# Strassen for the right half of two row blocks, streamed with B, and the loads and norms moved to make room

One Trainium2 chip, one core. The metric is the device time of one execution in microseconds (us), medians over runs. Engines go by the names that the profile gives them: PE does matrix products (TensorE), DVE and ACT work on vectors (VectorE and ScalarE), POOL and SP here mostly issue DMA transfers, that is loads and stores (GpSimd and SyncE). SBUF is the on-chip memory, PSUM the banks into which PE writes its products; copying a bank out to SBUF is called eviction. A norm is the work on a row block of A from its squares to its scale factor. Each normalized block is cast to fp16, then transposed. L and a number is a line of the kernel.

## The reference

```python
m, k, n = 2048, 2048, 2048          # a, b: float32 normal; gamma: float32; eps = 1e-5
x = np.matmul(a, b)
rms = np.sqrt(np.mean(x ** 2, axis=-1, keepdims=True) + eps)
return (gamma * x / rms).astype(np.float32)
```

## The kernel before

Rows are worked in 16 blocks of 128, columns in 4 chunks of 512. A matmul here is always one 128x128 stationary block against 512 columns, so a plain chunk of a row block costs 16 of them (the depth of 2048 in steps of 128).

- *Left half* (to about 39.8 us): row blocks 0 to 3 times the left 1024 columns, plainly, while A and the left half of B arrive in eight pieces. A PE transpose turns each piece of A.
- *Right half* (to about 69 us): the same four row blocks times the right 1024 columns, while the right half of B arrives. 4 rows x 2 chunks x 16 = 128 matmuls.
- *Groups*: the other 12 row blocks in pairs. A pair and two column chunks make a 2x2 problem with all of B in place, so one level of Strassen's scheme (7 products of half-size blocks in place of 8, at the price of extra sums) serves: 7 products of 8 matmuls, 56, in place of 64 plain ones. DVE makes the sums of A, of B and of the products; ACT evicts, squares, and normalizes the next blocks of A to fp16; DMA transposes those.

The stream of the right half and the list of loads of the kernel before:

```python
later = ([("b", kp) for kp in range(5)]                 # pieces of the right half of B
         + [("a", HB), ("b", 5), ("b", 6), ("a", HB + 1), ("b", 7)])   # and blocks 4, 5 of A
# ...
groups2 = [(r, c) for r in range(HB) for c in (2, 3)][:-1]   # 7 chunks stream, the 8th follows
for kp in range(KP):
    load_later(1)
    # ... transposes of block 4 in steps 6 and 7
    stream(groups2, kp, before)                 # 14 plain matmuls per piece of B
    square(squares[kp][0], x_chunk(*squares[kp]))
    # ... norm and fp16 of blocks 4, 5 after steps 4 and 6; sums of B for the groups
```

One product of a group, and the buffers: PSUM has 7 banks for these; a row's output lives in one of 8 SBUF buffers, reused group after group.

```python
p2, p5 = new_bank(), new_bank()
product(g, j, 2, p2)
nc.scalar.copy(out=c, in_=p2)          # c is in the output buffer: waits for its last store
product(g, j, 5, p5)
nc.vector.tensor_tensor(out=t, in0=p5, in1=c, op=ALU.add)
# ... product 1
product(g, j, 4, p2, start=False)      # goes on top of p2: waits for the copy
product(g, j, 3, p5, start=False)      # goes on top of p5: waits for the sum t
```

Of the kernel before, what the change touches and what calls it, by code (L numbers as in the profile page):

```python
# [17 lines left out]
def kernel(  # L18
# [13 lines left out]
    nc = tc.nc  # L32
# [18 lines left out]
    stat_pool = ctx.enter_context(tc.tile_pool(name="stat_pool", bufs=8))  # L51
# [25 lines left out]
    spare = head_at.rearrange("p t r m -> p (t r m)")[:, K:2 * K].bitcast(FP32)[:, 0:CH]  # L77

    def a16_slot(mb):

        if mb < HB + 2:
            return x_slot[HB + 1 + 2 * (mb % 2)].bitcast(FP16)
        flat = head_at.rearrange("p t r m -> p (t r m)").bitcast(FP16)
        return flat[:, (2 + mb % 2) * K:(3 + mb % 2) * K]
# [27 lines left out]

    def load_block(mb):
        a32[mb] = a_pool.tile([P, K], FP32, name="a32")
        nc.gpsimd.dma_start(out=a32[mb], in_=a[mb * P:(mb + 1) * P, :])
# [8 lines left out]
    identity_f = consts.tile([P, P], FP32, name="identity_f")  # L124
# [4 lines left out]
    nc.vector.memset(warm, 0.0)  # L129
    identity = consts.tile([P, P], BF16, name="identity")  # L130
# [43 lines left out]
    def transpose_half(mb, g):  # L174
        bank = ps_t.tile([P, CH], FP32, name="tbank")
# [7 lines left out]
        nc.vector.tensor_copy(out=at(mb)[:, g * 8:(g + 1) * 8, :], in_=view)  # L183
# [8 lines left out]
    def new_msq(mb):  # L192
        msq[mb] = stat_pool.tile([P, NCH + 1], FP32, name="msq")
        n_sq[mb] = 0

    for mb in range(HB):
        new_msq(mb)
        nc.gpsimd.memset(msq[mb][:, NCH:], float(eps))
# [27 lines left out]
    def row_apply(mb):  # L226
        a16[mb] = a16_slot(mb)
        if mb < HB + 2:
            nc.vector.tensor_scalar_mul(out=a16[mb], in0=a32.pop(mb), scalar1=factor.pop(mb))
# [5 lines left out]
    def quarter(g, r, c):  # L235
        return at(2 * g + r)[:, c::2, :]

    def a_sums(g, which):
# [3 lines left out]
        for s in which:  # L242
            x, y, op = terms[s]
            nc.vector.tensor_tensor(out=s_sum[s], in0=x, in1=y, op=op)  # L244
# [11 lines left out]
    def b_sum_7(j, kp):  # L256

        b21, b22 = (b_quarter(j, kp, 1, c) for c in range(2))
        nc.vector.tensor_tensor(out=b21, in0=b21, in1=b22, op=ALU.add)

    def b_sum_6(j, kp):

        b11, b12 = (b_quarter(j, kp, 0, c) for c in range(2))
        nc.vector.tensor_tensor(out=b12, in0=b12, in1=b11, op=ALU.add)

# [6 lines left out]
    def product(g, j, m, bank, start=True):  # L272
        for kp in range(KP):
            lhsT = {3: quarter(g, 0, 0), 4: quarter(g, 1, 1)}[m] if m in (3, 4) else s_sum[m]
            rhs = {1: lambda: sums[j][:, 0, kp, :], 2: lambda: b_quarter(j, kp, 0, 0),
                   3: lambda: sums[j][:, 1, kp, :], 4: lambda: sums[j][:, 2, kp, :],
                   5: lambda: b_quarter(j, kp, 1, 1), 6: lambda: b_quarter(j, kp, 0, 1),
                   7: lambda: b_quarter(j, kp, 1, 0)}[m]()
            nc.tensor.matmul(bank, lhsT[:, kp, :], rhs,  # L279
                             start=(start and kp == 0), stop=(kp == KP - 1),  # L280
                             skip_group_check=not start)
# [5 lines left out]
    def square(mb, src):  # L287
# [3 lines left out]
        nc.scalar.activation(out=sq[:, 0:CH], in_=src, func=ACTF.Square,  # L291
                             scale=inv_sqrt_n, accum_out=msq[mb][:, c:c + 1])
# [40 lines left out]

    def finish(mb, order=(0, 1)):
        if mb not in rms_of:
            take_rms(mb)
        r = inverse(rms_of.pop(mb))
        for h in order:
            x = x_half.pop((mb, h))
            nc.vector.scalar_tensor_tensor(  # L340
                out=x, in0=x, scalar=r, in1=gamma_sb[:, h * HALF:(h + 1) * HALF],
                op0=ALU.mult, op1=ALU.mult)
# [394 lines left out]
```

## Time and profile before

| | before |
|---|---|
| time, median (range) | 224.41 us (224.26 to 225.11) |
| span of the profiled run | 222.6 us |
| left half, right half, groups, tail (us, read from PE's timeline) | 7.7 to 39.84, to 69.25, to 214.7, to 222.6 |

The page of the kernel before: busy time of an engine, tenths of busy time in 40 slices of 5.6 us, and the chain that ended last.

```profile
...
PE 211.1 (95%) x1043; PEld 98.6 (44%) x1043; DVE 161.8 (73%) x324; ACT 129.1 (58%) x272; POOL 24.5 (11%) x49
...
PE   7899999999999999999999999999999999999950
...
DVE  2427557983999989978949298837994589587692
...
PE 83%; DMA 8%; DVE 2%; POOL 2%; issue 1%; ACT 1%; DVEq 0%; ACTq 0%; POOLq 0%
...
```

PE is full in nearly every slice and makes up 83% of the chain. But its busy share alone proves little: the mean matmul is shown as 379 ns long, though they start 216 ns apart. How long PE really idles is seen in the stretches and the timeline. The view by stretches (start:end, then busy us of PE, its weight load, DVE, ACT, POOL, and granted clock, DMA share, GB/s):

```profile
...
core 0: us, PE busy (x) PEld busy (x) DVE busy (x) ACT busy (x) POOL busy (x), PEclk, DMA share, GB/s
7.00:39.80 32.80, 31.84 (x190) 16.04 (x189) 18.37 (x39) 3.16 (x6) 11.33 (x17) 1.00 1.21 208
39.80:69.20 29.40, 29.40 (x161) 14.30 (x160) 24.18 (x59) 19.38 (x43) 2.34 (x4) 1.00 1.00 284
69.20:93.50 24.30, 24.30 (x113) 10.95 (x112) 22.90 (x49) 19.01 (x42) 1.24 (x3) 1.00 0.70 226
93.50:214.70 121.20, 121.18 (x570) 55.50 (x568) 91.52 (x169) 83.64 (x174) 3.71 (x9) 1.00 0.62 193
214.70:222.60 7.90, 0.00 (x0) 0.00 (x0) 3.26 (x7) 2.04 (x7) 0.00 (x0) 0.79 0.60 209
...
```

From 39.8 to 214.7 us the view shows no idle time on PE; in the last stretch (the tail) it has nothing left to do. The waits of PE inside the stream (for whom, total us, times, longest):

```profile
...
PE acc L350 <- DMA b<-in_b_dram: 0.4, 1, 0.4
PE tbank L382 <- DVE head_at L170: 0.4, 1, 0.4
```

0.8 us in all. PE's timeline (start, duration, line and operation, count):

```profile
...
39.84 19.80 PE L350 MATMUL acc<-b,head_at 128*128 128x512 bf16 x91
59.48 0.61 PE L179 MATMUL tbank<-identity_h,x 128*128 128x128 f16 x8
...
67.09 2.32 PE L350 MATMUL acc<-b,head_at 128*128 128x512 bf16 x10
69.25 3.62 PE L279 MATMUL acc<-b,s 128*128 128x512 bf16 x16
72.70 1.89 PE L279 MATMUL acc<-t_left,s 128*128 128x512 bf16 x8
...
212.77 1.91 PE L677 MATMUL acc<-b,s 128*128 128x256 bf16 x16
```

The 91 matmuls from 39.84 us end, start to start, at 59.48: 19.64/91 = 0.2158 us each. The last line is the last product. The Trainium skill's page "TensorE: Matmul & The Clock Gate", section "Back-to-back issue gap", gives about 216 ns for the isolated gap at 512 columns and about 131 ns as a sustained figure; this trace shows 216 in a stream without gaps, and 131 nowhere.

### The profile page before, as it was taken

How to read it: one execution, taken by the hardware profiler on the slowest of the kernel's cores; microseconds unless marked ns; L12 is line 12 of the kernel's file. 1: busy time of each engine (PE TensorE's matmuls, PEld its weight loads, DVE VectorE, ACT ScalarE, POOL GpSimd, SP SyncE). 2: the span in 40 equal slices, each digit the busy share in tenths (PEclk: the TensorE clock that was granted, in tenths of full speed). 3: DMA queues.
4: the chain of work that ended last, by engine and by line, in shares of the span. 5: the costliest groups of instructions: out<-in, count | busy, mean ns of one | idle time of the engine just before them, and what ended most of it. 6: DMA issues, size and time to landing. Idle time of an engine off the chain costs nothing.

```text
span 222.6 us, 3026 instructions
## 1 busy us (share of the span) xinstructions
PE 211.1 (95%) x1043; PEld 98.6 (44%) x1043; DVE 161.8 (73%) x324; ACT 129.1 (58%) x272; POOL 24.5 (11%) x49
## 2 busy tenths in 40 slices
PE   7899999999999999999999999999999999999950
PEld 2445444444454444444444444444444444444430
DVE  2427557983999989978949298837994589587692
ACT  3110002807698895799646985699478954334570
POOL 7534232300000001000100002000200000000000
PEclk9999999999999999999999999999999999999997
DMA  6999999999973499818889259945994794044045
GB/s 184 223 202 209 203 208 211 212 303 259 327 280 159 188 272 292 310 72 226 276 228 400 58 174 222 366 151 143 246 368 168 97 282 189 0 188 193 0 190 188
DMA packets 36176, 47.13 MB, mean 212 GB/s; under 512 B 21952, under 2 KB 26048, under 8 KB 34496
## 3 DMA queue, kind: packets, MB, share of 16 engines
q0 software_dynamic: 9648, 23.33, 41.6%
q1 hardware_dynamic: 26080, 22.29, 33.0%
q10 hardware_dynamic: 432, 1.31, 2.0%
q8 instruction: 8, 0.13, 0.2%
q14 instruction: 8, 0.07, 0.1%
HBM read 34.60 MB, written 16.78 MB: 231 GB/s over the span
## 4 chain that ended last, share of the span: by engine, by line
PE 83%; DMA 8%; DVE 2%; POOL 2%; issue 1%; ACT 1%; DVEq 0%; ACTq 0%; POOLq 0%
PE acc L279 63%; PE acc L350 18%; DMA b<-in_b_dram 8%; POOL early L106 1%; DVE x L617 1%; POOL b L100 1%; DVE x L620 1%; PE tbank L179 1%; PE tbank L382 1%; PE tbank L165 1%; ACT sq L291 0%; DVEq L732 0%; ACT sq L682 0%; DVE x L690 0%; DVE r L322 0%
## 5 line engine op out<-in xcount | busy, mean ns | idle before, releaser
L279 PE MATMUL acc<-b,s 128*128 128x512 bf16 x376 | 83.3, 379 | 0.0
L279 PEld LDWEIGHTS <-s 128*128 128x128 f16 x472 | 46.2, 98 | 55.7 <-DVE s L244 0.2
L350 PE MATMUL acc<-b,head_at 128*128 128x512 bf16 x240 | 55.1, 379 | 0.6 <-DMA b<-in_b_dram 0.4
L291 ACT ACTIVATE sq<-x 128x512 bf16<-128x512 f32 x62 | 39.1, 631 | 10.9 <-DVE x L520 5.1
L340 DVE SCALAR_TENSOR_TENSOR x<-x,r,gamma_sb 128x1024 f32<-128x1024 f32 x28 | 34.7, 1282 | 0.8
L209 ACT ACTIVATE sq<-a 128x1024 bf16<-128x1024 f32 x24 | 25.4, 1057 | 16.8 <-DMA a<-in_a_dram 16.4
L350 PEld LDWEIGHTS <-head_at 128*128 128x128 bf16 x240 | 22.9, 98 | 26.7 <-issue 1.1
L393 ACT COPY x<-acc 128x512 f32<-128x512 f32 x11 | 5.9, 591 | 25.1 <-PE acc L350 25.1
L231 ACT ACTIVATE head_at<-a,s 128x2048 f16<-128x2048 f32 x10 | 19.9, 1990 | 0.0
L279 PEld LDWEIGHTS <-at_even 128*128 128x128 f16 x96 | 9.4, 98 | 11.5 <-issue 0.4
L279 PEld LDWEIGHTS <-head_at 128*128 128x128 f16 x96 | 9.4, 98 | 11.3
L100 POOL DMA_DIRECT2D b<-in_b_dram x15 | 10.6, 708 | 16.0 <-DMA b<-in_b_dram 13.2
L217 DVE TENSOR_SCALAR s<-norm 128x1 f32<-128x1 f32 x12 | 1.8, 150 | 14.3 <-ACT norm L212 14.2
L244 DVE TENSOR_TENSOR s<-at_even 128x1024 f16<-128x1024 f16 x15 | 9.7, 684 | 2.8 <-DMA at_even<-head_at 2.8
L291 ACT ACTIVATION_READ_ACCUMULATOR sq<-x 128x1 f32 x62 | 11.7, 188 | 0.0
L279 PE MATMUL acc<-t_left,s 128*128 128x512 bf16 x48 | 11.3, 379 | 0.0
L279 PE MATMUL acc<-early,s 128*128 128x512 bf16 x48 | 11.3, 379 | 0.0
L279 PE MATMUL acc<-early,at_even 128*128 128x512 bf16 x48 | 11.0, 379 | 0.0
L279 PE MATMUL acc<-t_left,at_even 128*128 128x512 bf16 x48 | 10.9, 379 | 0.0
L509 ACT COPY x<-acc 128x512 f32<-128x512 f32 x10 | 5.7, 575 | 8.9 <-PE acc L279 8.9
L279 PE MATMUL acc<-t_left,head_at 128*128 128x512 bf16 x48 | 10.8, 379 | 0.0
L279 PE MATMUL acc<-early,head_at 128*128 128x512 bf16 x48 | 10.8, 379 | 0.0
(86 smaller groups left out, 205.8 us busy)
## 6 DMA issues: line engine op xcount, KB each, us to landing
out_dram<-x SPq DMA_DIRECT2D x30, 512.0 KB, 3.1
a<-in_a_dram POOLq DMA_DIRECT2D x12, 1024.0 KB, 8.5
b<-in_b_dram POOLq DMA_DIRECT2D x15, 512.0 KB, 17.1
early<-in_a_dram POOLq DMA_DIRECT2D x7, 256.0 KB, 14.8
early<-in_b_dram ACTq DMA_DIRECT2D x2, 512.0 KB, 5.9
gamma_sb<-in_gamma_dram POOLq DMA_DIRECT2D x1, 1024.0 KB, 19.9
out_dram<-x SPq DMA_DIRECT2D x3, 256.0 KB, 3.5
early<-in_a_dram SPq DMA_DIRECT2D x1, 512.0 KB, 5.7
```

Of the source, the lines that this page charges most:

```text
L100: nc.gpsimd.dma_start(out=raw[j][kp], in_=b[kp * W2:(kp + 1) * W2, j * HALF:(j + 1) * HALF].rearrange("(t p) n -> p t n", p=P))
L106: nc.gpsimd.dma_start(out=ah(kp), in_=a[0:HB * P, kp * W2:(kp + 1) * W2].rearrange("(r p) k -> p r k", p=P))
L165: nc.tensor.matmul(view[:, t, r, :], ah(kp)[:, r, t * P:(t + 1) * P], identity, is_transpose=True, start=(t == 0 and r == 0), stop=(t == 1 ...
L209: nc.scalar.activation(out=junk, in_=a32[mb][:, h * HALF:(h + 1) * HALF], func=ACTF.Square, scale=2.0 ** -8, accum_out=n2[:, h:h + 1])
L231: nc.scalar.activation(out=a16[mb], in_=a32.pop(mb), func=ACTF.Copy, scale=factor.pop(mb))
L244: nc.vector.tensor_tensor(out=s_sum[s], in0=x, in1=y, op=op)
L279: nc.tensor.matmul(bank, lhsT[:, kp, :], rhs, start=(start and kp == 0), stop=(kp == KP - 1), skip_group_check=not start)
L291: nc.scalar.activation(out=sq[:, 0:CH], in_=src, func=ACTF.Square, scale=inv_sqrt_n, accum_out=msq[mb][:, c:c + 1])
L340: nc.vector.scalar_tensor_tensor(out=x, in0=x, scalar=r, in1=gamma_sb[:, h * HALF:(h + 1) * HALF], op0=ALU.mult, op1=ALU.mult)
L350: nc.tensor.matmul(bank, head_at[:, kt, r, :], head_rhs(c, kt), start=(kt == 0), stop=(kt == KT - 1))
L393: copy(out=x_chunk(*g), in_=banks[g])
L509: nc.scalar.copy(out=x21, in_=p2)
```

## The change

The intent: treat row blocks 2 and 3 as a pair already in the right half. Its products 2, 5 and 1 stream with B beside the plain chunks of blocks 0 and 1; products 4, 3, 7 and 6 follow (the turn from the stream to the groups). That is 56 matmuls for the 64 of before. All else makes room: sums of A and B move into the left half; blocks 4 and 5 load after all of B; one square root at the start puts the table load of ACT there; block 8 loads ahead of row block 2's stores and block 9 behind; in later groups the norms move behind the group's first copy. The first group now does product 5 ahead of product 2. The core of the diff (cut; each piece under @@ is shortened):

```diff
-    later = ([("b", kp) for kp in range(5)]
-             + [("a", HB), ("b", 5), ("b", 6), ("a", HB + 1), ("b", 7)])
+    later = [("b", kp) for kp in range(KP)] + [("a", n) for n in range(4)]   # halves of 4, 5
@@ start
+    nc.vector.memset(pace, 1.0)
+    nc.scalar.activation(out=pace, in_=pace, func=ACTF.Sqrt)
@@ left half, each step
+        if kp in early_sums:
+            before.append(lambda: a_sums(PAIR, *early_sums[kp]))
+        if 0 < kp < KP - 2:
+            b_sums_in_place(0, kp - 1)
@@ right half
-    groups2 = [(r, c) for r in range(HB) for c in (2, 3)][:-1]
+    plain = [(r, c) for r in range(2) for c in (2, 3)]
+    def stream_right(kp):            # (cut) 8 plain matmuls, then
+            for m in (2, 5):
+                pair_matmul(m, kp)
+            if kp > 0:
+                pair_matmul(1, kp - 1)
@@ after it
+    product(PAIR, 1, 4, pair[2], start=False)
+    row_norm(HB)
+    row_norm(HB + 1)
+    # (cut) product 3
+    product(PAIR, 1, 7, p7, within={5: [lambda: turn(HB, 0)]})   # transposes of block 4
+    turn(HB, 1)
+    product(PAIR, 1, 6, p6)
+    # (cut) transposes of block 5; the pair's last four additions go into the first group
@@ first group, right half
             if g + 2 < NG:
                 hook(0, load_after, g, nxt + 2)
-                hook(0, load_block, nxt + 3)
-                hook(5, row_norm, nxt + 2)
+                if g == G0:
+                    hook(2, wait_for, x_slot[HB + r2][:, 0:1])
+                    hook(2, load_block, nxt + 3)
+                    hook(5, row_norm, nxt + 2)
+                else:
+                    hook(0, load_block, nxt + 3)
@@ later groups
-                hook(0, row_factor, nxt)
-                hook(1, apply, nxt)
+                    hook(1, row_norm, nxt)
+                hook(2, row_factor, nxt)
+                hook(2, apply, nxt)
```

More of the change, by code (lines that the diff above doesn't have):

```diff
@@ L50 @@
     sq_pool = ctx.enter_context(tc.tile_pool(name="sq_pool", bufs=1))
-    stat_pool = ctx.enter_context(tc.tile_pool(name="stat_pool", bufs=8))
+    stat_pool = ctx.enter_context(tc.tile_pool(name="stat_pool", bufs=4))
+    msq_pool = ctx.enter_context(tc.tile_pool(name="msq_pool", bufs=8))
     ps_t = ctx.enter_context(tc.tile_pool(name="ps_t", bufs=1, space=bass.MemoryType.PSUM))
@@ L75 @@
     x_slot = [consts.tile([P, HALF], FP32, name=f"x_{n}") for n in range(8)]
-    spare = head_at.rearrange("p t r m -> p (t r m)")[:, K:2 * K].bitcast(FP32)[:, 0:CH]
+    spare = head_at.rearrange("p t r m -> p (t r m)")[:, K:2 * K].bitcast(FP32)
+    spare = [spare[:, 0:CH], consts.tile([P, CH], FP32, name="t_first")]
     def a16_slot(mb):
-        if mb < HB + 2:
-            return x_slot[HB + 1 + 2 * (mb % 2)].bitcast(FP16)
         flat = head_at.rearrange("p t r m -> p (t r m)").bitcast(FP16)
@@ L111, with load_half @@
     a32 = {}
+    def load_half(mb, h):
+        if h == 0:
+            a32[mb] = a_pool.tile([P, K], FP32, name="a32")
+        nc.gpsimd.dma_start(out=a32[mb][:, h * HALF:(h + 1) * HALF],
+                            in_=a[mb * P:(mb + 1) * P, h * HALF:(h + 1) * HALF])
     def load_block(mb):
@@ L123 @@
     load_head(1)
-    identity_f = consts.tile([P, P], FP32, name="identity_f")
+    identity_f = t_left[:, 2, KP - 1, 0:2 * P].bitcast(FP32)
     make_identity(nc, identity_f)
@@ L172, with transpose_half @@
     a16 = {}
-    def transpose_half(mb, g):
-        bank = ps_t.tile([P, CH], FP32, name="tbank")
+    def transpose_half(mb, g, own_bank):
+        if own_bank:
+            bank = ps_t.tile([P, CH], FP32, name="tbank")
+        else:
+            bank = ps_a.tile([P, CH], FP32, name="acc")
         view = bank.bitcast(FP16).rearrange("p (g m) -> p g m", m=P)
@@ L182, in transpose_half, with take_transposed @@
             )
-        nc.vector.tensor_copy(out=at(mb)[:, g * 8:(g + 1) * 8, :], in_=view)
+        return view
+    def take_transposed(mb, g, view, copy):
+        copy(out=at(mb)[:, g * 8:(g + 1) * 8, :], in_=view)
     def transpose_dma(mb):
@@ L192, in new_msq @@
     def new_msq(mb):
-        msq[mb] = stat_pool.tile([P, NCH + 1], FP32, name="msq")
+        msq[mb] = msq_pool.tile([P, NCH + 1], FP32, name="msq")
         n_sq[mb] = 0
@@ L197 @@
         new_msq(mb)
+        nc.gpsimd.memset(msq[mb][:, NCH - 1:NCH], 0.0)
         nc.gpsimd.memset(msq[mb][:, NCH:], float(eps))
@@ L235, in quarter, with sum_of, a_sums @@
     def quarter(g, r, c):
+        if g < G0:
+            return head_at[:, c::2, 2 * g + r, :]
         return at(2 * g + r)[:, c::2, :]
-    def a_sums(g, which):
+    def sum_of(g, s):
+        return s_sum[s].bitcast(BF16) if g < G0 else s_sum[s]
+    def a_sums(g, which, lo=0, hi=KP):
         a11, a12, a21, a22 = (quarter(g, r, c) for r in range(2) for c in range(2))
@@ L243, in a_sums @@
             x, y, op = terms[s]
-            nc.vector.tensor_tensor(out=s_sum[s], in0=x, in1=y, op=op)
+            nc.vector.tensor_tensor(out=sum_of(g, s)[:, lo:hi, :], in0=x[:, lo:hi, :],
+                                    in1=y[:, lo:hi, :], op=op)
     def b_quarter(j, kp, r, c):
@@ L254, in b_sums @@
             nc.vector.tensor_tensor(out=sums[j][:, n, kp, :], in0=x, in1=y, op=op)
-    def b_sum_7(j, kp):
-        b21, b22 = (b_quarter(j, kp, 1, c) for c in range(2))
-        nc.vector.tensor_tensor(out=b21, in0=b21, in1=b22, op=ALU.add)
-    def b_sum_6(j, kp):
-        b11, b12 = (b_quarter(j, kp, 0, c) for c in range(2))
-        nc.vector.tensor_tensor(out=b12, in0=b12, in1=b11, op=ALU.add)
     def b_sums_in_place(j, kp):
@@ L270, in b_sums_in_place, with product_matmul, product @@
                                 op=ALU.add)
-    def product(g, j, m, bank, start=True):
-        for kp in range(KP):
-            lhsT = {3: quarter(g, 0, 0), 4: quarter(g, 1, 1)}[m] if m in (3, 4) else s_sum[m]
-            rhs = {1: lambda: sums[j][:, 0, kp, :], 2: lambda: b_quarter(j, kp, 0, 0),
-                   3: lambda: sums[j][:, 1, kp, :], 4: lambda: sums[j][:, 2, kp, :],
-                   5: lambda: b_quarter(j, kp, 1, 1), 6: lambda: b_quarter(j, kp, 0, 1),
-                   7: lambda: b_quarter(j, kp, 1, 0)}[m]()
-            nc.tensor.matmul(bank, lhsT[:, kp, :], rhs,
-                             start=(start and kp == 0), stop=(kp == KP - 1),
-                             skip_group_check=not start)
+    def product_matmul(g, j, m, bank, kp, start=True):
+        lhsT = {3: quarter(g, 0, 0), 4: quarter(g, 1, 1)}[m] if m in (3, 4) else sum_of(g, m)
+        rhs = {1: lambda: sums[j][:, 0, kp, :], 2: lambda: b_quarter(j, kp, 0, 0),
+               3: lambda: sums[j][:, 1, kp, :], 4: lambda: sums[j][:, 2, kp, :],
+               5: lambda: b_quarter(j, kp, 1, 1), 6: lambda: b_quarter(j, kp, 0, 1),
+               7: lambda: b_quarter(j, kp, 1, 0)}[m]()
+        nc.tensor.matmul(bank, lhsT[:, kp, :], rhs,
+                         start=(start and kp == 0), stop=(kp == KP - 1),
+                         skip_group_check=not start)
+    def product(g, j, m, bank, start=True, within={}):
+        for kp in range(KP):
+            for work in within.get(kp, ()):
+                work()
+            product_matmul(g, j, m, bank, kp, start)
     x_half = {}
@@ L291, in square, with square_half @@
         nc.scalar.activation(out=sq[:, 0:CH], in_=src, func=ACTF.Square,
+                             scale=inv_sqrt_n, accum_out=msq[mb][:, c:c + 1])
+    def square_half(mb, h):
+        c = n_sq[mb]
+        n_sq[mb] += 1
+        sq = sq_pool.tile([P, 2 * CH], BF16, name="sq")
+        nc.scalar.activation(out=sq, in_=x_tile(mb, h), func=ACTF.Square,
                              scale=inv_sqrt_n, accum_out=msq[mb][:, c:c + 1])
@@ L332, in rows, with scale, store @@
         return out[mb * P:(mb + 1) * P, lo:hi]
+    inverse_of = {}
+    def scale(mb, order=(0, 1)):
+        if mb not in inverse_of:
+            if mb not in rms_of:
+                take_rms(mb)
+            inverse_of[mb] = inverse(rms_of.pop(mb))
+        for h in order:
+            x = x_half[mb, h]
+            nc.vector.scalar_tensor_tensor(
+                out=x, in0=x, scalar=inverse_of[mb], in1=gamma_sb[:, h * HALF:(h + 1) * HALF],
+                op0=ALU.mult, op1=ALU.mult)
+    def store(mb, order=(0, 1)):
+        for h in order:
+            nc.sync.dma_start(out=rows(mb, h * HALF, (h + 1) * HALF), in_=x_half.pop((mb, h)))
     def finish(mb, order=(0, 1)):
-        if mb not in rms_of:
-            take_rms(mb)
-        r = inverse(rms_of.pop(mb))
         for h in order:
-            x = x_half.pop((mb, h))
-            nc.vector.scalar_tensor_tensor(
-                out=x, in0=x, scalar=r, in1=gamma_sb[:, h * HALF:(h + 1) * HALF],
-                op0=ALU.mult, op1=ALU.mult)
-            nc.sync.dma_start(out=rows(mb, h * HALF, (h + 1) * HALF), in_=x)
+            scale(mb, (h,))
+            store(mb, (h,))
     def head_rhs(c, kt):
@@ L361, in load_later @@
             kind, which = later.pop(0)
-            load_b(1, which) if kind == "b" else load_block(which)
+            load_b(1, which) if kind == "b" else load_half(HB + which // 2, which % 2)
     def stream(groups, kp, before=(), when=None):
@@ L393, in evict @@
             copy(out=x_chunk(*g), in_=banks[g])
+    PAIR = G0 - 1
     groups1 = [(r, c) for r in range(HB) for c in range(2)][:-1]
@@ L399 @@
         x_tile(r, 0)
+    early_sums = {4: ((2,), 0, 6), 5: ((5,), 0, 7), 6: ((1,), 0, KP)}
     transpose_first()
@@ L412 @@
             b_sums(0, kp - 1)
+        if 0 < kp < KP - 2:
+            b_sums_in_place(0, kp - 1)
     load_later(2)
-    b_sums(0, KP - 1)
-    def prepare(mb):
-        row_norm(mb)
-        row_factor(mb)
-        row_apply(mb)
-    def b_sums_2(kp):
-        b_sums_in_place(0, kp)
-        b_sums(1, kp)
-        if kp + 1 < KP:
-            b_sum_7(1, kp)
-    r3 = HB - 1
-    squares = groups1 + [last1]
-    groups2 = [(r, c) for r in range(HB) for c in (2, 3)][:-1]
+    squares = groups1 + [last1]
@@ new lines, with pair_matmul @@
+    plain = [(r, c) for r in range(2) for c in (2, 3)]
+    pair = {}
+    def pair_matmul(m, kp):
+        if kp == 0:
+            pair[m] = new_bank()
+        product_matmul(PAIR, 1, m, pair[m], kp)
+    def stream_right(kp):
+        order = [(g, kt) for kt in (2 * kp, 2 * kp + 1) for g in plain]
+        if kp in (0, KP - 1):
+            order.sort(key=lambda x: plain.index(x[0]))
+        if kp == KP - 1:
+            for m in (2, 5):
+                pair_matmul(m, kp)
+            pair_matmul(1, kp - 1)
+        for g, kt in order:
+            if kt == 0:
+                banks[g] = new_bank()
+            head_matmul(banks[g], *g, kt)
+        if kp < KP - 1:
+            for m in (2, 5):
+                pair_matmul(m, kp)
+            if kp > 0:
+                pair_matmul(1, kp - 1)
+        else:
+            pair_matmul(1, kp)
@@ L431 @@
     for kp in range(KP):
         load_later(1)
-        before = [lambda: transpose_half(HB, 0)] if kp == 6 else []
-        if kp == 7:
-            before = [lambda: transpose_half(HB, 1)]
-        stream(groups2, kp, before)
+        b_sums(1, kp)
+        stream_right(kp)
         square(squares[kp][0], x_chunk(*squares[kp]))
-        if kp == 4:
-            prepare(HB)
-        if kp == 6:
-            prepare(HB + 1)
-        elif kp == KP - 1:
-            b_sums_in_place(0, kp - 1)
-        else:
-            b_sums_2(kp)
+        if kp > 0:
+            b_sums_in_place(1, kp - 1)
@@ L447 @@
+        if kp == 0:
+            b_sums(0, KP - 1)
+            b_sums_in_place(0, KP - 3)
+        if kp == 1:
+            b_sums_in_place(0, KP - 2)
+            b_sums_in_place(0, KP - 1)
+        if kp == 2:
+            a_sums(PAIR, (2,), 6, KP)
+            a_sums(PAIR, (5,), 7, KP)
+        if kp in (3, 4):
+            a_sums(PAIR, ((7, 6)[kp - 3],))
     nc.gpsimd.dma_start(out=gamma_sb, in_=gamma.partition_broadcast(P))
@@ L449, with turn, pair_sums, pair_ends @@
     load_block(HB + 3)
-    def squares2(r):
-        for c in (2, 3):
-            square(r, x_chunk(r, c))
-    evict(groups2[0:2], ())
-    squares2(0)
-    evict(groups2[2:-1], ())
-    bank = new_bank()
-    for kt in range(KT):
-        if kt in (0, 6):
-            transpose_half(HB + 1, kt // 6)
-            if kt == 0:
-                b_sums(1, KP - 2)
-                b_sum_7(1, KP - 2)
-        head_matmul(bank, r3, 3, kt)
-    evict(groups2[-1:], ())
-    row_norm(HB + 2)
-    a_sums(G0, (2, 5, 1))
-    finish(0, (1, 0))
-    b_sums_2(KP - 1)
-    nc.scalar.copy(out=x_chunk(r3, 3), in_=bank)
-    squares2(1)
+    r2, r3 = HB - 2, HB - 1
+    for r in range(HB):
+        x_tile(r, 1)
+    x11, x12, x21, x22 = (x_chunk(r, c) for r in (r2, r3) for c in (2, 3))
+    nc.scalar.copy(out=x22, in_=pair[2])
+    nc.vector.tensor_tensor(out=x22, in0=pair[5], in1=x22, op=ALU.add)
+    evict(plain, (2, 3))
+    b_sums_in_place(1, KP - 1)
+    product(PAIR, 1, 4, pair[2], start=False)
+    row_norm(HB)
+    row_norm(HB + 1)
+    nc.vector.tensor_tensor(out=x22, in0=pair[1], in1=x22, op=ALU.subtract)
+    row_factor(HB)
+    product(PAIR, 1, 3, pair[5], start=False)
+    row_apply(HB)
+    nc.scalar.copy(out=x21, in_=pair[2])
+    row_factor(HB + 1)
+    row_apply(HB + 1)
+    p7 = new_bank()
+    turned = {}
+    def turn(mb, g):
+        turned[mb, g] = transpose_half(mb, g, g == 0)
+    product(PAIR, 1, 7, p7, within={5: [lambda: turn(HB, 0)]})
+    turn(HB, 1)
+    for g in range(2):
+        take_transposed(HB, g, turned[HB, g], nc.scalar.copy)
+    nc.scalar.copy(out=x12, in_=pair[5])
+    p6 = new_bank()
+    product(PAIR, 1, 6, p6)
+    a_sums(G0, (5,))
+    for g in range(2):
+        turn(HB + 1, g)
+        take_transposed(HB + 1, g, turned[HB + 1, g], nc.vector.tensor_copy)
+    square_half(0, 1)
+    square_half(1, 1)
+    take_rms(0)
+    a_sums(G0, (2, 1))
+    def pair_sums():
+        nc.vector.tensor_tensor(out=x11, in0=x22, in1=x21, op=ALU.add)
+        nc.vector.tensor_tensor(out=x22, in0=x22, in1=x12, op=ALU.add)
+    def pair_ends():
+        nc.vector.tensor_tensor(out=x11, in0=p7, in1=x11, op=ALU.add)
+        nc.vector.tensor_tensor(out=x22, in0=p6, in1=x22, op=ALU.add)
     late = []
@@ L491, in group_half @@
         x11, x12, x21, x22 = (x_chunk(ra, c1), x_chunk(ra, c2), x_chunk(rb, c1), x_chunk(rb, c2))
-        t = x22
+        first = (g, j) == (G0, 0)
+        c, t = spare if first else (x22, x22)
         at_hook(0)
         p2, p5 = new_bank(), new_bank()
-        product(g, j, 2, p2)
-        c = spare if (g, j) == (G0, 0) else t
-        nc.scalar.copy(out=c, in_=p2)
+        one, two = ((5, p5), (2, p2)) if first else ((2, p2), (5, p5))
+        product(g, j, *one)
+        nc.scalar.copy(out=c, in_=one[1])
         last_squares()
         at_hook(1)
-        product(g, j, 5, p5)
-        nc.vector.tensor_tensor(out=t, in0=p5, in1=c, op=ALU.add)
+        product(g, j, *two)
+        nc.vector.tensor_tensor(out=t, in0=two[1], in1=c, op=ALU.add)
         at_hook(2)
@@ L529, in load_after @@
     def load_after(g, mb):
-        wait_for(x_chunk(2 * g + 1, 1)[:, 0:1])
+        wait_for(at(2 * g + 3)[:, KT - 1, 0:1] if g == G0 else x_chunk(2 * g + 1, 1)[:, 0:1])
         load_block(mb)
@@ L550, in hooks_of @@
             if g == G0:
-                hook(0, row_factor, nxt)
-                hook(1, row_norm, nxt + 1)
-                hook(1, apply, nxt)
+                hook(0, finish, 0, (1,))
+                hook(1, row_norm, nxt)
+                hook(1, take_rms, 1)
+                hook(2, row_factor, nxt)
+                hook(2, finish, 0, (0,))
+                hook(2, apply, nxt)
+                hook(2, row_norm, nxt + 1)
                 hook(2, a_sums, g, (7, 6))
+                hook(2, finish, 1, (1, 0))
                 hook(2, row_factor, nxt + 1)
-                hook(2, finish, 1)
-                hook(3, squares2, 2)
+                hook(2, pair_sums)
+                hook(2, pair_ends)
                 hook(4, apply, nxt + 1)
-                hook(4, finish, 2)
-                hook(6, b_sum_7, 1, KP - 1)
+                hook(7, square_half, r2, 1)
             else:
                 done = [2 * g - 2, 2 * g - 1]
-                hook(0, row_factor, nxt)
-                hook(1, apply, nxt)
+                if g == G0 + 1:
+                    done.insert(0, r3)
+                else:
+                    hook(1, row_norm, nxt)
+                for mb in done:
+                    hook(1, take_rms, mb)
+                hook(2, row_factor, nxt)
+                hook(2, apply, nxt)
                 if g == G0 + 1:
                     hook(2, finish, r3)
-                    done.insert(0, r3)
-                for mb in done:
-                    hook(1, take_rms, mb)
-                hook(1, row_norm, nxt + 1)
-                hook(2, row_factor, nxt + 1)
-                hook(4 if g == G0 + 1 else 3, finish, 2 * g - 2)
+                hook(2, row_norm, nxt + 1)
+                hook(3, scale, 2 * g - 2)
+                hook(3, row_factor, nxt + 1)
                 hook(4, apply, nxt + 1)
+                hook(4, store, 2 * g - 2)
         else:
             if g == G0:
-                hook(1, squares2, r3)
-                for kp in range(KP):
-                    hook(2, b_sum_6, 1, kp)
+                hook(1, take_rms, r2)
+                hook(1, square_half, r3, 1)
+                hook(2, finish, r2, (1, 0))
             else:
@@ L586, in hooks_of @@
                 hook(0, load_after, g, nxt + 2)
-                hook(0, load_block, nxt + 3)
-                hook(5, row_norm, nxt + 2)
+                if g == G0:
+                    hook(2, wait_for, x_slot[HB + r2][:, 0:1])
+                    hook(2, load_block, nxt + 3)
+                    hook(5, row_norm, nxt + 2)
+                else:
+                    hook(0, load_block, nxt + 3)
         return hooks
```

## The prediction

> **What bounds it.** The tensor engine. Windows view: PE busy 31.8 of the 32.8 us from 7.0 to 39.8 us, every us from 39.8 to 214.7, idle for the last 7.9. The timeline has 7 matmuls of 128x512 in 1.51 us: 216 ns each. That is the isolated gap (about 216 ns for N=512) of the Trainium skill's page "TensorE: Matmul & The Clock Gate", section "Back-to-back issue gap"; the 131 ns it gives as sustained is not seen here. The waits view has only 0.8 us of PE waiting inside the stream (0.44 for a piece of B, 0.35 for a transpose).
>
> **What the change does to PE.** The right half of row blocks 2, 3 costs 64 matmuls before, 7 x 8 = 56 after. Transposes and later groups stay. So 8 x 0.216 = 1.73 us go, all on the critical path: 222.7 is the floor. Start and tail are untouched.
>
> **What could give it back** (pitches from the back-to-back timeline: three B sums 1.0 us, in-place sum or A sum 0.6, fp32 add or eviction 0.6, scaled output half 1.2, A block to fp16 1.2, norm of a block on ACT 2.6):
> 1. Left half: DVE gets 0.6 (in-place) plus up to 0.6 (A sum) per step: 2.2 becomes 3.4 of 3.9 us. Fits.
> 2. Right half: a step is 11 matmuls = 2.38 us, was 14 = 3.02. A block of B lands every 2.49 us from 38.8 us on; with blocks 4, 5 moved behind B the eighth lands near 56.2, PE wants it at 56.25. DVE's 17 us of work there end near 58, in time. Zero margin: 0 to 0.5 us of PE waiting for B.
> 3. Turn to the pair's last products (59 to 68 us): block 4's halves land near 57.5 and 58.7, norm by 61, fp16 by 63.4, PE wants to transpose at 63.6. Block 5 has 1 us to spare. The sum for the next group's second product comes within 0.1 us of its need.
> 4. First group, left: the pair's last sums stand behind three output halves on DVE, so its product-7 bank is freed near 81.1; PE wants it at 81.5.
> 5. Block 8 lands near 93; ACT must copy the next group's first product by 97.2: 0.6 us to spare.
> Everything fits, barely; I add 0.4 us of small waits. From 98 us on PE had no wait, so moving norms there is worth nothing.
>
> **Predicted: 223.1 us, 222.3 to 225.0 in 8 of 10.** Faster by over 2%: 1%. Within 2%: 95%. Slower by over 2%: 4%.
>
> **What would show each step.** 8 fewer 128x512 matmuls, last matmul 1.2 to 1.7 us earlier, tail near 7.9 us. First group's first product starts near 67.6 to 68.0 (before 69.25). PE's waits on B in the right half under 0.5 us in sum. No PE gap over 0.3 us at pair product 7 and the transposes of block 4, none over 0.5 at the second product of the first group's right half (it waits for the pair's last sum). DVE near 100% from 38 to 90 us.
>
> **What would make it wrong.** B arriving slower than one block per 2.49 us: every 0.1 us adds 0.7 of PE waiting, and the norms of blocks 4, 5 are late as well. DVE instructions queueing behind a wait for ACT (norm, rms) between 61 and 82 us: each 1 us of delay beyond 0.5 goes into PE. Late transposes by DMA of blocks 6, 7. Four waits of 0.5 us cancel the gain; over 2% needs a load or a norm late by whole microseconds.

## The result, and the profile after

| | before | after |
|---|---|---|
| median (range), us | 224.41 (224.26 to 225.11) | 222.83 (222.51 to 222.88) |
| ratio, 95% interval | | 0.9925 (0.9908 to 0.9941) |
| span of the profiled run, us | 222.6 | 221.1 |

A ratio here is the mean time of one kernel's fast runs over the mean of the other's fast runs of the same rounds, so it is not quite the ratio of the medians quoted beside it. The time fell by 1.6 us, 0.75%: sure, and under 2%.

The page after, the lines that answer to those of before:

```profile
...
PE 210.4 (95%) x1035; PEld 97.7 (44%) x1035; DVE 167.9 (76%) x330; ACT 128.0 (58%) x263; POOL 26.7 (12%) x56
...
PE   7999999999999999999999999999999999999950
...
DVE  2428789999978898969696649855794759797691
...
PE 69%; DMA 23%; DVE 2%; POOL 2%; issue 1%; ACT 1%; DVEq 0%; ACTq 0%; POOLq 0%
...
```

DVE is fuller in slices 4 to 10. In the chain the loads of B have grown from 8% to 23%: before, the chain entered PE at 24.6 us; now it runs through the arrival of B up to 56.4 us. The stretches after (bounds moved with the stages):

```profile
...
7.00:39.80 32.80, 31.86 (x190) 15.93 (x189) 23.48 (x47) 3.32 (x6) 11.62 (x17) 1.00 1.21 208
39.80:67.70 27.90, 27.68 (x152) 13.26 (x150) 26.09 (x63) 16.26 (x35) 3.19 (x6) 1.00 0.94 250
67.70:91.90 24.20, 24.20 (x117) 10.93 (x115) 22.64 (x42) 20.18 (x41) 2.28 (x4) 1.00 0.77 244
91.90:213.20 121.30, 121.23 (x570) 55.51 (x568) 90.99 (x170) 84.14 (x175) 3.71 (x9) 1.00 0.63 201
213.20:221.10 7.90, 0.00 (x0) 0.00 (x0) 3.22 (x7) 2.02 (x6) 0.00 (x0) 0.80 0.59 205
...
```

The right half with its turn (second line) takes 27.9 us where it took 29.4, with 0.2 us of PE idle; DVE is nearly full there (26.1 us). The stages behind it are as long as before: 24.2 and 121.3 us, and 7.9 us of tail. PE's waits after:

```profile
...
PE acc L384 <- DMA b<-in_b_dram: 0.5, 1, 0.5
PE tbank L415 <- DVE head_at L177: 0.4, 1, 0.4
PE acc L289 <- DMA b<-in_b_dram: 0.2, 1, 0.2
```

PE's timeline after, right half and turn:

```profile
...
39.68 1.89 PE L384 MATMUL acc<-b,head_at 128*128 128x512 bf16 x8
...
55.87 0.38 PE L289 MATMUL acc<-early,s 128*128 128x512 bf16 x1
56.47 0.59 PE L289 MATMUL acc<-b,s 128*128 128x512 bf16 x2 [0.22 <-DMA b<-in_b_dram]
...
62.51 1.24 PE L289 MATMUL acc<-b,s 128*128 128x512 bf16 x5
63.63 0.62 PE L189 MATMUL tbank<-identity_h,head_at 128*128 128x128 f16 x8
...
67.80 3.72 PE L289 MATMUL acc<-b,s 128*128 128x512 bf16 x16
71.36 1.89 PE L289 MATMUL acc<-t_left,s 128*128 128x512 bf16 x8
...
```

And the last product:

```profile
...
211.22 1.91 PE L769 MATMUL acc<-b,s 128*128 128x256 bf16 x16
```

How to read it, start to start. A step of the right half is 11 matmuls, 2.37 us. In the last one PE waits for B: the matmul at 55.87 should be followed at 56.09, and is at 56.47. So 0.38 us are lost, though the waits view says 0.2: a matmul is drawn 163 ns longer than its place in the stream, which hides that much of every gap. The first group starts at 67.80 instead of 69.25. The last product starts at 211.22 instead of 212.77, 1.55 earlier:

| part, start to start | us |
|---|---|
| 8 matmuls fewer, 8 x 0.2158 | -1.73 |
| wait for the last piece of B | +0.38 |
| wait for block 4's fp16 (63.59 wanted, 63.63) | +0.04 |
| first group's second product waits for its sum (67.80 to 71.36; before 69.25 to 72.70) | +0.11 |
| two small waits of before in the groups that are gone (140.07 us to the last product, now 139.86) | -0.21 |
| right half starts earlier (39.68, before 39.84); differs between profiles of one kernel as well (39.90 below) | -0.16 |
| sum (the rest is rounding) | -1.57 |

### The profile page after: what moved, and what is told of

The parts are those of the page before. It is cut to its first block, busy times and chain, and to the rows that moved or that the text cites. A ratio compares the mean times of both kernels' runs of the same rounds, so it can differ in the third digit from the quotient of the medians.

```text
span 221.1 us, 3017 instructions
## 1 busy us (share of the span) xinstructions
PE 210.4 (95%) x1035; PEld 97.7 (44%) x1035; DVE 167.9 (76%) x330; ACT 128.0 (58%) x263; POOL 26.7 (12%) x56
## 4 chain that ended last, share of the span: by engine, by line
PE 69%; DMA 23%; DVE 2%; POOL 2%; issue 1%; ACT 1%; DVEq 0%; ACTq 0%; POOLq 0%
PE acc L289 67%; DMA b<-in_b_dram 23%; DVE x L709 1%; POOL early L105 1%; DVE x L712 1%; PE acc L384 1%; POOL b L99 1%; ACT sq L307 0%; PE tbank L189 0%; PE acc L189 0%; DVEq L824 0%; ACT sq L774 0%; DVE x L782 0%; DVE r L345 0%; ACT rms L351 0%
## 5 line engine op out<-in xcount | busy, mean ns | idle before, releaser
L289 PE MATMUL acc<-b,s 128*128 128x512 bf16 x408 | 92.1, 379 | 0.2 <-DMA b<-in_b_dram 0.2
L289 PEld LDWEIGHTS <-s 128*128 128x128 f16 (+1 forms) x512 | 49.9, 98 | 60.3 <-issue 0.5
L384 PE MATMUL acc<-b,head_at 128*128 128x512 bf16 x176 | 41.8, 379 | 0.6 <-DMA b<-in_b_dram 0.5
L307 ACT ACTIVATE sq<-x 128x512 bf16<-128x512 f32 x54 | 34.0, 630 | 6.9 <-DVE x L709 3.0
L384 PEld LDWEIGHTS <-head_at 128*128 128x128 bf16 x176 | 16.8, 98 | 20.1 <-issue 1.2
L289 PEld LDWEIGHTS <-head_at 128*128 128x128 f16 (+1 forms) x112 | 10.9, 98 | 13.2
L289 PE MATMUL acc<-early,head_at 128*128 128x512 bf16 x64 | 14.5, 379 | 0.0
L264 DVE TENSOR_TENSOR s<-head_at 128x1024 f16<-128x1024 f16 (+5 forms) x22 | 13.4, 635 | 0.1
L596 DVE TENSOR_TENSOR x<-x,x 128x512 f32<-128x512 f32 x9 | 6.2, 692 | 8.8 <-ACT x L594 8.3
L280 DVE TENSOR_TENSOR b<-b 128x1024 bf16<-128x1024 bf16 x16 | 10.8, 686 | 0.2
```

The lines of the kernel that those rows point to most:

```text
L264: nc.vector.tensor_tensor(out=sum_of(g, s)[:, lo:hi, :], in0=x[:, lo:hi, :], in1=y[:, lo:hi, :], op=op)
L280: nc.vector.tensor_tensor(out=flat[:, 1:3, :], in0=flat[:, 1:3, :], in1=flat[:, 0::3, :], op=ALU.add)
L289: nc.tensor.matmul(bank, lhsT[:, kp, :], rhs, start=(start and kp == 0), stop=(kp == KP - 1), skip_group_check=not start)
L307: nc.scalar.activation(out=sq[:, 0:CH], in_=src, func=ACTF.Square, scale=inv_sqrt_n, accum_out=msq[mb][:, c:c + 1])
L384: nc.tensor.matmul(bank, head_at[:, kt, r, :], head_rhs(c, kt), start=(kt == 0), stop=(kt == KT - 1))
L596: nc.vector.tensor_tensor(out=t, in0=t, in1=x12, op=ALU.add)
```

## The experiments

All are edits of the changed kernel, and all gave correct results. Times of the first and last set were taken beside runs of the kernel before with median 224.54 us, of the middle set (0 and 5 to 7) with 224.2. Ratios are to the kernel before; the changed kernel's own are 0.9925 and, measured again, 0.9921.

**0. The changed kernel again.**

> The changed kernel again, to stand beside the three of this call: 222.8 us, ratio to before 0.9925 plus or minus 0.0015.

222.48 us, ratio 0.9921 (0.9909 to 0.9933). As expected. In this profile the right half starts at 39.90, 0.2 later, and the wait for the last piece of B is not there. PE's timeline at the place that had 0.38 us of gap:

```profile
...
56.09 0.38 PE L289 MATMUL acc<-early,s 128*128 128x512 bf16 x1
56.31 0.59 PE L289 MATMUL acc<-b,s 128*128 128x512 bf16 x2
...
```

0.22 us from one to the other is one matmul. (The trace that was kept of this run is of another execution; it has 56.23 and 56.45, no wait either.) It isn't PE's start alone that decides. Run 8 below came to the same place at the same time as the profile with the gap, and did not wait:

```profile
...
55.86 0.38 PE L289 MATMUL acc<-early,s 128*128 128x512 bf16 x1
56.08 0.59 PE L289 MATMUL acc<-b,s 128*128 128x512 bf16 x2
...
```

What differs is the load. The last piece of B took 20.2 us from issue to landing in the profile with the gap (36.25 to 56.4, wanted at 56.09), 19.7 in run 8. In the kept profiles of this run and of runs 1, 3 to 6, 8 and 9, which load B and use it in the same order, it took 19.6 to 19.9 us, and none has a gap of more than 0.02 us there. So PE and the loads do run a close race, but 0.38 us is the outlier among these nine, not the rule.

**1. Product 6 twice: as many matmuls as before the change.**

```diff
     product(PAIR, 1, 6, p6)
+    product(PAIR, 1, 6, p6)
```

> The changed kernel, with the pair's product 6 computed twice into the same bank: 8 matmuls of 128x512 more, so as many as before the change, all else as changed. Result stays right. Theory (the gain is the 8 matmuls and nothing else): first group starts 1.7 us later (69.5 us, changed kernel 67.8), the 0.1 us wait for the second product's sum goes, time 222.8 + 1.6 to 1.7 = 224.4 to 224.6, that is the kernel before. Rival (the gain came with the moved loads and norms): those are still in, so the time stays below 223.6.

224.24 us, ratio 0.9991 (0.9973 to 1.0008): the time of the kernel before. PE's timeline has the doubled product and the first group's start at 69.20:

```profile
...
64.85 3.62 PE L289 MATMUL acc<-b,s 128*128 128x512 bf16 x16
...
69.20 3.73 PE L289 MATMUL acc<-b,s 128*128 128x512 bf16 x16
...
```

So with everything else of the change in place, 8 matmuls are worth 0.66% or 1.5 us, and that is the whole gain within the noise: by the interval of the ratio, at most 0.27% or 0.6 us is left for the moved loads and norms. The rival, under 223.6 us, falls. The first group starts 1.4 us later than in the changed kernel's profile and not 1.73, since that profile has the 0.38 us wait for B and this one hasn't. The 0.1 us at the second product, which I expected to go, stayed (the 16 matmuls still take 3.56 us): its sum waits for copies of block 5's transposes, which moved along.

**2. Blocks 4 and 5 loaded between pieces of B, as before.**

```diff
-    later = [("b", kp) for kp in range(KP)] + [("a", n) for n in range(4)]
+    later = ([("b", kp) for kp in range(5)]
+             + [("a", HB), ("b", 5), ("b", 6), ("a", HB + 1), ("b", 7)])
@@ (cut) and each of the two blocks is loaded whole, no longer in halves
```

> The changed kernel with blocks 4 and 5 loaded where the kernel before loaded them: between pieces 4 and 5, and 6 and 7 of the right half of B. Theory (after the change PE eats B exactly as fast as it arrives, so order of arrival is on the path): each block of A pushes B back by 2.45 us, so the last piece lands 4.9 us later (near 61.2 instead of 56.3). PE waits in the right half grow from 0.4 to about 5.2 us start to start, nearly all of it lost: time 222.8 + 4.5 to 4.9 = 227.3 to 227.7. Rival (there is slack to hide a late piece of B): under 224.5.

227.59 us, ratio 1.0159 (1.0108 to 1.021; one of the four runs was at 229.84). Waits of PE:

```profile
...
PE acc L289 <- DMA b<-in_b_dram: 2.7, 1, 2.7
PE acc L384 <- DMA b<-in_b_dram: 2.5, 2, 1.9
...
```

4.8 us over the changed kernel. In the kernel before this order left PE no wait for B in the right half (its one wait for B, 0.4 us, is at 24.7 us, in the left half), when a step lasted 3.02 us and a piece came each 2.49; with steps of 2.37 us it decides.

**3. No square root at the start.**

```diff
-    nc.scalar.activation(out=pace, in_=pace, func=ACTF.Sqrt)
```

> The changed kernel without the square root on one column at the very start, so that the table of square roots is loaded (1.28 us in both traces) at its first real use, as in the kernel before, where it was off the path. Theory (the turn to the pair's last products has no slack): the load falls between the squares and the norm of block 4, near 61.1; norm and fp16 block 4 come 1.28 us later, PE, which wanted the block at 63.6, stands about 1.0 to 1.2 us and nothing gives it back: time 222.8 + 0.9 to 1.3 = 223.7 to 224.1. Rival (slack as in the kernel before): within 0.2 of 222.8.

223.74 us, ratio 0.9968 (0.9953 to 0.9983). ACT's timeline between the squares and the norm of block 4:

```profile
...
60.83 1.28 ACT L225 ACT_TABLE_LOAD   x1
62.13 0.30 ACT L225 ACTIVATE norm<-n 128x1 f32<-128x1 f32 x1
...
```

and PE's, at the transposes of block 4:

```profile
...
64.50 0.62 PE L188 MATMUL tbank<-identity_h,head_at 128*128 128x128 f16 x8 [0.98 <-DVE head_at L243]
...
```

0.98 us of visible gap is 1.15 us start to start (five matmuls from 62.27 end at 63.35), and 0.9 us of time. (The changed kernel's profile has the 0.38 us wait for B and this one hasn't, so the two need not be equal.) The cast to fp16 ended at 64.44 here and at 63.57 in the changed kernel, each 0.06 us before PE's transposes, so this cast is what PE waits for. In the kernel before, the same table load sat at 53.55 us and nothing waited for it. The page "ScalarE: Activation LUTs" of the Trainium skill, section "What ACT_TABLE_LOAD costs", gives 1283 ns for the load, as both traces do, and 2.66 us in all with a drain. Here ACT's instruction before the load ended at 60.81, the load began at 60.83 and the norm 1.30 us later: no drain is seen on either side of it.

**4. One needless sum on DVE ahead of the pair's last additions.**

```diff
+        nc.vector.reduce_sum(out=held, in_=gamma_sb[:, 0:HALF], axis=mybir.AxisListType.X)
         # then pair_sums, pair_ends
```

> The changed kernel with one needless sum over 1024 columns (about 1.1 to 1.2 us of DVE, written to a column nobody reads) ahead of the pair's last sums in the first group. Theory (the bank of the pair's product 7 is freed 0.3 us before PE wants it for the second product of the right half; traced 81.3 against 81.6): PE stands 0.8 to 1.0 us there, and the time is 222.8 + 0.7 to 1.0 = 223.5 to 223.8. Rival (DVE has slack there, since it only falls behind and catches up): within 0.2 of 222.8.

222.94 us, ratio 0.9931 (0.9916 to 0.9946). The expectation fell: no gap at the second product. The built program shows why. PSUM banks are given out when the kernel is built, it seems in the order in which the builder expects them to come free. With the extra sum it gave the second product (number 5) of the right half the bank that ACT frees, and the pair's bank to product 1, which wants it 1.7 us later. (In the changed kernel product 5 is in bank 2, that of the pair's product 7; here it is in bank 7 and product 1 in bank 2.) The timeline has another trace of the delay, 3.84 us instead of 3.62 for the 16 matmuls of products 4 and 3: product 3 waited 0.2 us for the sum of the first two. The delay was 1.13 us of DVE, so the slack is about 0.9 us, and another wait sets it. The changed kernel's own trace agrees: the sum of the first two products ended at 85.93, and product 3 began at 86.90. That led to the next run.

**8. Two such sums.**

> As the run with one needless sum on DVE ahead of the pair's last sums, now with two. That run fell short of its expectation: building the kernel anew gave the second product another bank (the one freed first) and the pair's bank to the product after it, which wants it 1.7 us later. New theory: DVE's slack there is about 0.9 us, set by the sum of the right half's first two products, which must be done before product 3 reuses the bank (in the run with one delay it came 0.2 us late). Two delays add 1.13 us more, so PE stands 1.2 to 1.4 us ahead of product 3: time 1.1 to 1.4 over the changed kernel. Rival (DVE's lateness is never paid there): within 0.3 of the changed kernel.

224.2 us, ratio 0.9988 (0.9969 to 1.0007), 1.4 us over the changed kernel. PE's timeline, right half of the first group: products 1, 4, 3:

```profile
...
83.34 1.89 PE L289 MATMUL acc<-early,s 128*128 128x512 bf16 x8
85.06 1.89 PE L289 MATMUL acc<-early,at_even 128*128 128x512 bf16 x8
87.97 1.89 PE L289 MATMUL acc<-early,at_even 128*128 128x512 bf16 x8 [1.02 <-DVE x L587]
...
```

Product 3 waits 1.02 us for the sum on DVE, as the new theory has it; another 0.3 us goes just ahead of the first line, where product 1 now does wait for the pair's bank (31 of the 32 matmuls before it were recorded; 83.34 where 83.06 follows from 76.15).

**5. Norms, factors and outputs of the later groups where they stood before.**

```diff
-                    hook(1, row_norm, nxt)
-                hook(2, row_factor, nxt)
-                hook(2, apply, nxt)
+                hook(0, row_factor, nxt)
+                hook(1, apply, nxt)
@@ (cut) the next block's norm, the row factors and the output stores go back too
@@ right half of a group
-                    hook(5, row_norm, nxt + 2)
@@ (cut)
+                hook(5, row_norm, nxt + 2)
```

> The changed kernel with the norms, factors and outputs of the later groups where they stood before the change (norm of the next block at the end of the group before). Theory (PE has no wait from 98 us on in either trace, so their place there is worth nothing): within 0.3 us of the changed kernel. Rival (the moved norms are part of the gain): slower by 0.5 us or more.

222.73 us, ratio 0.993 (0.9916 to 0.9945), beside 222.48 and 0.9921 for the changed kernel: 0.25 us between the medians, with overlapping intervals. In the profile PE has no wait from 98 us on. Worth nothing, as far as five rounds can tell.

**6. Blocks 8 and 9 both ahead of row block 2's stores.**

```diff
-        wait_for(at(2 * g + 3)[:, KT - 1, 0:1] if g == G0 else x_chunk(2 * g + 1, 1)[:, 0:1])
+        wait_for(x_chunk(2 * g + 1, 1)[:, 0:1])
@@
-                    hook(2, wait_for, x_slot[HB + r2][:, 0:1])
-                    hook(2, load_block, nxt + 3)
@@ (cut)
+                hook(0, load_block, nxt + 3)
```

> The changed kernel with blocks 8 and 9 loaded together behind the first group's left half, as before the change, both ahead of row block 2's stores. Theory (worth nothing: the norm of block 8 comes out in time either way, block 8's load starts about 1 us earlier and the two stores come later): within 0.3 us of the changed kernel. Rival (loads and stores collide and PE waits): slower by 0.5 us or more.

224.59 us, ratio 1.0008 (0.9994 to 1.0022), 2.1 us over the changed kernel: all of the gain gone. I had expected nothing. PE's timeline, at products 4 and 3 of the second group:

```profile
...
97.89 1.89 PE L289 MATMUL acc<-t_left,head_at 128*128 128x512 bf16 x8 [0.84 <-ACT x L578]
100.44 1.89 PE L289 MATMUL acc<-t_left,head_at 128*128 128x512 bf16 x8 [0.66 <-DVE s L231]
...
```

and ACT's, at the copy of that group's first product:

```profile
...
97.25 0.58 ACT L578 COPY x<-acc 128x512 f32<-128x512 f32 x1 [3.76 <-DMA out_dram<-x]
...
```

The copy writes into the buffer whose content (row block 2) is still being stored. The view of transfers from 86 to 98 us shows the two stores (count, KB each, median us from issue to landing) in this run:

```profile
...
out_dram<-x SPq DMA_DIRECT2D x2, 512.0 KB, 9.7
```

and in the changed kernel, where ACT made the same copy without a wait for a store:

```profile
...
out_dram<-x SPq DMA_DIRECT2D x2, 512.0 KB, 6.5
...
94.74 0.57 ACT L578 COPY x<-acc 128x512 f32<-128x512 f32 x1
...
```

The stores share the transfer engines with two loads of 1 MB issued ahead of them. That agrees with the page "DMA: Bandwidth & Descriptors" of the Trainium skill, section "Issuing engines are not separate DMA queues": transfers run on the same 16 engines whoever issues them. The stores are issued by SP and the loads by POOL, and still 6.5 us became 9.7. Before the change the same two loads were issued together at 88.37 us with no such wait, since row block 2 was done earlier and its stores, issued at 84.70, went ahead of both: its outputs were scaled 13.9 us after the first group's start (83.19 to 69.25), now 18.8 us after it (86.56 to 67.80). The Strassen pair finishes last of all, and that moved the store into the loads.

**7. Three small waits taken off.**

```diff
+            pair_matmul(1, kp - 1)         # last step: needs no new piece of B
             for m in (2, 5):
                 pair_matmul(m, kp)
-            pair_matmul(1, kp - 1)
@@
+    row_norm(HB)                           # ahead of two evictions on ACT
     evict(plain, (2, 3))
-    row_norm(HB)
@@
-    take_rms(0)
-    a_sums(G0, (2, 1))
+    a_sums(G0, (2,))
+    take_rms(0)
+    a_sums(G0, (1,))
```

> The changed kernel with three of its waits taken off: in the last step of the right half the matmul that needs no new piece of B goes first; the norm of block 4 goes ahead of two evictions on ACT; the sum for the first group's second product goes ahead of the reduction for row block 0. Theory: PE's 0.38 us at the last piece of B shrinks by one matmul, 0.22, and the 0.1 us at the second product goes: 0.2 to 0.35 us under the changed kernel. Rival (some later wait with as little slack eats it): under 0.1 us.

222.76 us, ratio 0.9928 (0.9915 to 0.9941), no better than the changed kernel. The rival's number holds, though not by its reason. The wait for B was hardly there to be removed: none in the profile of run 0, and in this run's own the last piece landed at 56.42, about 0.15 us after the old order would have wanted it (56.27). And the second product still came 0.1 us late: with the reduction out of the way, DVE's sum began at 68.67, 0.04 before the 68.71 of run 0, because it needs the copy just ahead of it. I found no version that beats the changed kernel.

**9. Both blocks behind the outputs.**

```diff
-                hook(0, load_after, g, nxt + 2)
                 if g == G0:
                     hook(2, wait_for, x_slot[HB + r2][:, 0:1])
+                    hook(2, load_block, nxt + 2)
                     hook(2, load_block, nxt + 3)
@@ (cut) in the later groups load_after stays
```

> The changed kernel with blocks 8 and 9 both loaded behind row block 2's outputs. With both ahead the stores landed 2.4 us later, ACT waited for the row's buffer and PE for ACT. Theory (each of the two loads has one right side): block 8 lands near 94, its norm is done at 96.6 and ACT's copy of the next group's first product comes at 97.1, when PE wants it: 0 to 0.6 us over the changed kernel. Rival (only the stores matter, so block 8 may go behind as well): within 0.1 of it.

225.97 us, ratio 1.0059 (1.004 to 1.0078), 3.1 us over the changed kernel. ACT's timeline at the norm of block 8:

```profile
...
95.58 1.06 ACT L223 ACTIVATE sq<-a 128x1024 bf16<-128x1024 f32 x1 [5.73 <-DMA a<-in_a_dram]
...
```

Right in kind, much too small in size. Block 8 landed at 95.5 us, not 94, and ACT, in order, held back the copy that PE waits for (1.65 us there, 0.67 at the next product). So three orders of these two loads and the stores differ by up to 3.1 us, and the change has the best of them.

**10. Three companions taken back at once (2, 3 and 6 together).**

> The changed kernel with three of its companions taken back at once: blocks 4, 5 loaded between pieces of B (alone plus 4.7 us), no square root at the start (alone plus 0.9), blocks 8 and 9 both ahead of the stores (alone plus 2.1). Theory (they hit different places in time, so their costs add, but the table load and the late B overlap: with B 4.7 us late, blocks 4 and 5 are long there): 5.5 to 7.5 over the changed kernel, ratio to before 1.018 to 1.027, so the 8 matmuls alone would have been a loss. Rival (one wait hides another): under 5.0.

230.96 us, ratio 1.0283 (1.0257 to 1.031). That is 3.6% or 8.0 us over the changed kernel; alone they cost 4.8, 0.9 and 2.1, together 7.8. They add, within the noise, and the result is above the 5.5 to 7.5 us expected. I had expected the late B to hide the table load; it does not, since ACT takes up the norm of block 4 only after the last evictions, however long the block has been there, and PE's gap at block 4's transposes was 0.98 us again.

## Why the prediction was right

The predicted 223.1 us is 0.3 from the measured 222.83, and the range 222.3 to 225.0 holds it. The mechanism, eight matmuls off the path and small waits given back, is the one that run 1 shows. That the point came so near is in part luck: of the waits, the largest term is an outlier, and two terms that the prediction did not have (0.21 and 0.16 us) went the other way.

- *Left half: the new sums fit on DVE*: right. DVE's busy time rose from 18.4 to 23.5 us of 32.8, and PE's stayed (31.84, now 31.86).

- *8 x 0.216 = 1.73 us, all on the path*: right. Run 1 gives back 1.5 us for those 8 matmuls alone.
- *0 to 0.5 us of waiting for B, zero margin*: right. 0.38 us start to start in one profile, at most 0.02 in those of eight other runs with this order, and run 2 shows 4.8 us when pieces 5 to 8 come late.
- *The turn has no slack*: right. Block 4 was wanted at 63.59 and used at 63.63; 1.28 us of table load made a gap of 1.15 us and cost 0.9 us of time (run 3). The prediction did not name the early square root as the part of the change that made this fit.
- *0.4 us of small waits*: 0.38 + 0.04 + 0.11 = 0.53 came in the profiled run, and 0.21 of old ones went, which was not foreseen. The net is 0.32 there, and near 0 in a run without the outlier. The size is right only by luck.
- *The pair's bank is freed at 81.1, wanted at 81.5*: the times were nearly right (81.3 and, counted in matmuls from 76.54, 81.7), the conclusion that this is the tight place was wrong. The bank is assigned at build time and evades a delay; the tight place is the sum ahead of product 3, with about 0.9 us (runs 4 and 8).
- *Block 8: 0.6 us to spare*: mis-sized and incomplete. Block 8 landed at 92.2 us, not 93, and ACT's copy was done at 95.3 against 97.2: nearly 2 us. But the step looked only at the load, not at the store that must leave the copy's buffer first; run 6 puts 2.1 us on that.
- *Moving norms from 98 us on is worth nothing*: no gain was resolved (run 5).
- *DVE near 100% from 38 to 90 us*: 94% in both stretches (26.1 of 27.9 and 22.6 of 24.2 us).

What stays open: whether norms moved alone cost or bring 0.2 us, why PE's right half starts some tenths of a us earlier in some profiles, and why the last piece of B took 20.2 us in one of them.

## What to carry to other kernels

Count matmuls first: on a PE that hardly idles, the gain is their number times their spacing, known before anything is built; moving other work can add no more than the waits that PE still has (0.8 us in this stream). Then ask of everything PE will now reach earlier (a load, a table, a norm, a store that frees a buffer) when it is ready, since the eight matmuls were worth 1.5 us, and taking back three of the moves that let them count cost 8.0. Place loads and stores by who waits for them; and when an experiment shifts something, check the rebuilt program for what else the builder moved, such as PSUM banks.

## What the Trainium skill lacked or had wrong

- "TensorE: Matmul & The Clock Gate", section "Back-to-back issue gap": 131 ns as the sustained spacing at 512 columns is not seen; 91 matmuls in a row with weight loads took 215.8 ns each, the figure it calls isolated.
- "ScalarE: Activation LUTs", section "What ACT_TABLE_LOAD costs": 1283 ns is confirmed; the drain that makes it 2.66 us is not seen in run 3 (load 0.02 us after the end of ACT's instruction before it, norm 1.30 us after the load's start).
- "TensorE: Matmul & The Clock Gate" has formulas for both lengths of a matmul, but neither it nor another page says that their difference hides part of a gap in a profile: 379 ns drawn, 216 ns spaced, so a gap of 0.38 us shows as 0.22.
- "DMA: Bandwidth & Descriptors" gives no figure for a store against loads: stores of 512 KB took 6.5 us with one load of 1 MB issued ahead of them and one behind, and 9.7 us with both ahead.
